# A hybrid attention, RWKV and mixture-of-experts block on one core: the output projection in another order, loads in pieces, and the experts' first weights on GpSimd's queue

## The chip, the cores and the metric

The kernel runs on one core of a Trainium2 chip. The metric is the device time of one execution in microseconds (us). It is measured from outside; a profiled execution also has a span, from its first to its last instruction, which is a little shorter than its own time.

## The reference

One layer of a streaming encoder, for 256 tokens of 2048 channels, all in float32:

```
h = rms_norm(x, g_mix);  proj = h @ w_in                       # 2048 -> 4176 + 3360 columns
y_dsa  = sparse attention (8 heads x 128): an indexer scores all keys, each query keeps
         the best 64 admissible ones, softmax over them       # head outputs h0..h7
y_rwkv = RWKV-7 (16 heads x 64): token shift, decay, delta-rule scan over the 256 tokens,
         group norm, bonus, gate                              # blocks of two heads: r0..r7
x = x + concat(y_dsa, y_rwkv) @ w_out                          # the output projection, 2048 x 2048
t = rms_norm(x, g_ffn)
route: softmax over 4 groups, the best one; softmax over its 4 experts, the best two
y = sum over the 16 experts of weight * (silu(t @ w_gate) * (t @ w_up)) @ w_down   # hidden width 512
return x + y
```

The experts' weights are 16 x 3 matrices of 4 MB, 201 MB in all. The weights of the other stages are some 80 MB.

## The kernel before

**Matmuls in two parts.** Weights come from HBM as float32. For the two big projections each 128 x 512 tile is split into a high part (ScalarE, line 205, "ACT W L205") and a low part (VectorE, line 206, "DVE W L206"), and three matmuls are made of it (high x high, high x low, low x high). All matmuls are issued on line 130, so the trace tells them apart by the tiles' names: `pp` is a bank of the two big projections, `W` the split weights, `RA` and `RB` the raw weights as loaded, `yT` the inputs of the output projection.

**The stream.** The two big projections are one list of steps, `stream`. A step takes one split tile. `drive` (line 393) walks through the list in order: it loads raw weights some steps ahead (`load_raw`, line 187, 512 KB for two steps, three places to hold them), splits them up to three steps ahead, waits until the inputs that the step needs are planned (`od.need`), and emits the step's matmuls. A step of the output projection has 6 matmuls of 128 x 512. Its list is 4 chunks of 512 output columns (cc 0 to 3) with 16 steps each; step c of a chunk takes the channels in place c of `YSLOTS`, so it needs that head's or block's output, put there by `put_y` (line 887). Each chunk holds two of the four `pp` banks from its first step to the addition of x (`u_chain`, line 1126).

**The planner.** `Order` (line 44) keeps a clock of its own, in planned TensorE time. The work beside the stream, such as the early and late part of each RWKV block, the attention and the indexer, is written as generators that give a delay or an event's name where they must wait. Between two steps of the stream `run_ready` lets every generator go on whose time has come. If a step needs something that isn't planned yet, `od.need` moves the clock forward and takes from the generators alone, with no step in between. This fixes TensorE's order of instructions. The other engines' and queues' order is made by the framework's scheduler.

**One RWKV block b.** `rwkv_early` makes the block's matrices and starts `solve` (line 645): GpSimd writes them to HBM, reads them back as `at` in another layout in one 512 KB transfer, solves in 31 pairs of instructions (lines 655 and 657), and sends the result through HBM to `XT`. `rwkv_late` (line 663) needs that, holds a lock so that only one block is in its late part, and ends in `put_y(r b)`. Block 7's late part comes last.

**The start.** xT (x transposed) is loaded in pieces on SyncE's queue, with the first weights between, then all of x in one 2 MB transfer into `xt_` (line 261). ScalarE sums the squares (line 276); the reciprocal root spread over partitions is `rsB` (made with a matmul, `rps`), by which each block's outputs are scaled in `shift`.

**The experts' weights.** They are loaded as 192 chunks of 1 MB in the order of use. The first 23 go, as memory comes free, to places that the earlier stages used: 3 in `G` after block 7's early part, 6 after block 7's late part ("rw closed"), 6 after `enter_moe` (line 1013), which follows the last step of cc 0, 4 in the places of `yT` as cc 3 comes to its end, then 1 in the raw place, 2 in the places of `W`, and the rest later. `prefetch_step` (line 1116) spreads chunks 4 to 14 over the stream: with each raw load of two steps 1/2.2 of a chunk falls due. `load_chunk(i, True)` first makes a one-element copy on GpSimd that reads the weights just split (line 1089), so that the load can't start ahead of its turn. All chunk loads are issued on SyncE (line 1092), as are the raw weights; x for the residual (`uu`, line 1011) and the router's constants are issued on GpSimd. The ring holds 20 chunks and, at first, 3 more; after that `ahead` loads a chunk each time one has been used.

**After the projection.** The router's small operations follow (lines 1191 to 1264); two of its copies are on GpSimd (lines 1223 and 1236). Then the experts, two at a time in 8 turns: `gate`, `up` and `pd` matmuls, a `sc` matmul that scatters the result, and an addition into x1, which goes out.

## Time and profile before

| | us |
|---|---|
| median of 3 runs (1102.21 to 1104.61) | 1102.25 |
| the profiled execution's own time | 1108.09 |
| its span | 1106.1 |
| TensorE busy in the span, as the records show it | 1034.8 (94%) |
| VectorE, ScalarE, GpSimd busy | 535.7, 384.0, 258.6 |
| bytes moved | 298.74 MB, 270 GB/s over the span |
| weights of the experts begin to be used | at 650.55 |

The profiled execution took 5.84 us more than the median of the runs. Matmuls are pipelined and their ends are modelled, so a busy TensorE isn't TensorE at its peak: its pace is read from how many matmuls stand in a stretch. "Granted clock" is the share of TensorE's full 2.4 GHz; 0.5 is its lower level of 1.2 GHz, and a value between is a mean over both.

### The profile page before, as it was taken

What the parts mean: (1) busy time and instruction counts of PE and PEld (TensorE: products, weight loads), DVE (VectorE), ACT (ScalarE), POOL (GpSimd) and SP (SyncE); (2) the same over time, 40 slices, a digit from 0 to 9 for tenths busy, and PEclk for the clock granted to TensorE, in tenths of its full rate; (3) what the DMA queues carried; (4) which work ended last, traced back from release to release, by engine and by line L of the source; (5) the groups of instructions that cost most, each with busy time, mean ns of one, the idle gap of its engine ahead of it and who ended that gap; (6) DMA issues with size and microseconds to landing.
All of it is one profiled execution on the core that took longest, in us unless ns stands there. A gap on an engine that the chain in (4) does not pass through costs nothing.

```text
span 1106.1 us, 17189 instructions
## 1 busy us (share of the span) xinstructions
PE 1034.8 (94%) x6466; PEld 698.7 (63%) x6466; DVE 535.7 (48%) x1193; ACT 384.0 (35%) x816; POOL 258.6 (23%) x666
## 2 busy tenths in 40 slices
PE   5999999989899999898799789999999999999996
PEld 5999888967698877686577654444444343434342
DVE  5887668777768776855354231313121313121212
ACT  6666555646446564644244211000000101010101
POOL 1416572648346535353110100000000000000000
PEclk9999999999999998998799899999999999999998
DMA  8566554454345543445299969999999999999995
GB/s 317 166 187 191 162 153 150 124 140 127 118 141 181 161 143 101 141 124 207 72 331 330 394 252 364 364 420 420 420 421 421 420 420 419 421 420 420 420 417 202
DMA packets 62266, 298.74 MB, mean 270 GB/s; under 512 B 9040, under 2 KB 12928, under 8 KB 37856
## 3 DMA queue, kind: packets, MB, share of 16 engines
q1 hardware_dynamic: 56720, 289.29, 69.6%
q0 software_dynamic: 5456, 8.28, 3.1%
q8 instruction: 53, 0.87, 0.3%
q14 instruction: 37, 0.30, 0.1%
HBM read 294.37 MB, written 3.15 MB: 269 GB/s over the span
## 4 chain that ended last, share of the span: by engine, by line
PE 77%; DMA 7%; DVE 5%; ACT 4%; POOL 3%; issue 2%; SPq 1%; ACTq 0%; DVEq 0%; POOLq 0%
PE pp L130 27%; PE pd L130 10%; PE gate L130 10%; PE up L130 10%; PE misc L130 6%; DMA RA<-wo 4%; PE sc L130 3%; PE pz L130 2%; DVE W L206 2%; PE py L130 2%; DMA xt__114<-x 1%; POOL xt L657 1%; ACT W L205 1%; POOL tt L655 1%; PE pc L130 1%
## 5 line engine op out<-in xcount | busy, mean ns | idle before, releaser
L130 PE MATMUL pp<-W,hT 128*128 128x512 f32 x768 | 194.3, 405 | 6.5 <-DVE W L206 6.5
L206 DVE TENSOR_TENSOR W<-RA,W 128x512 fp32r<-128x512 f32 x200 | 137.5, 697 | 98.9 <-ACT W L205 97.0
L130 PE MATMUL pp<-hT,W 128*128 128x256 f32 x1296 | 174.0, 292 | 11.8 <-ACT W L205 10.5
L130 PEld LDWEIGHTS pp<-hT,W 128*128 128x128 f32 x1296 | 164.5, 197 | 15.7 <-ACT W L205 10.7
L205 ACT CAST W<-RA 128x512 fp32r<-128x512 f32 x200 | 122.1, 619 | 133.5 <-PE pp L130 87.6
L130 PEld LDWEIGHTS pp<-W,hT 128*128 128x128 f32 x768 | 144.4, 193 | 38.0 <-DVE W L206 7.4
L130 PE MATMUL pp<-W,yT 128*128 128x512 f32 x384 | 99.5, 414 | 13.7 <-ACT yT L890 6.6
L655 POOL TENSOR_TENSOR tt<-xt,at 128x24 f32<-128x24 f32 (+23 forms) x248 | 89.6, 361 | 72.8 <-DMA at<-din 54.1
L130 PEld LDWEIGHTS pp<-W,yT 128*128 128x128 f32 x384 | 74.4, 198 | 34.0 <-ACT W L205 8.0
L657 POOL TENSOR_TENSOR xt<-xt,tt 128x24 f32<-128x24 f32 (+23 forms) x248 | 89.1, 359 | 19.3
L206 DVE TENSOR_TENSOR W<-RB,W 128x512 fp32r<-128x512 f32 x100 | 68.7, 695 | 38.8 <-ACT W L205 38.3
L130 PE MATMUL pd<-ew,R 128*64 128x512 f32 x352 | 81.1, 598 | 2.7 <-ACT R L1376 2.7
L205 ACT CAST W<-RB 128x512 fp32r<-128x512 f32 x100 | 61.0, 619 | 60.4 <-PE pp L130 45.5
L130 PE MATMUL up<-ew,R 128*64 128x512 f32 x352 | 79.3, 592 | 0.0
L130 PEld LDWEIGHTS misc<-sel,uu 128*128 128x128 f32 x512 | 59.6, 192 | 15.2 <-issue 13.8
L1386 ACT ACTIVATE Y<-pd,sv 128x512 fp32r<-128x512 f32 x32 | 22.0, 688 | 126.8 <-PE pd L130 126.8
L1387 DVE SCALAR_TENSOR_TENSOR Y<-pd,sv,Y 128x512 fp32r<-128x512 f32 x32 | 24.0, 751 | 83.0 <-ACT Y L1386 83.0
L130 PE MATMUL misc<-sel,uu 128*128 128x128 f32 x512 | 63.0, 278 | 0.7 <-DVE sel L1308 0.7
L1396 DVE TENSOR_TENSOR x<-x,sc 128x512 f32<-128x512 f32 x56 | 36.0, 685 | 54.9 <-PE sc L130 54.9
L130 PE MATMUL gate<-ew,R 128*64 128x512 f32 x272 | 61.7, 595 | 0.0
L1318 DVE TENSOR_TENSOR R<-misc,gF 128x512 f32<-128x512 f32 x28 | 19.4, 691 | 79.5 <-PE misc L130 79.5
L130 PEld LDWEIGHTS up<-ew,R 128*64 128x64 f32 x352 | 25.3, 137 | 50.2 <-issue 49.4
(371 smaller groups left out, 1217.2 us busy)
## 6 DMA issues: line engine op xcount, KB each, us to landing
ew<-we SPq DMA_DIRECT2D x91, 1024.0 KB, 19.1
ew<-wdn SPq DMA_DIRECT2D x40, 1024.0 KB, 17.7
ewh<-we SPq DMA_DIRECT2D x24, 1024.0 KB, 17.4
RA<-wd SPq DMA_DIRECT2D x43, 512.0 KB, 3.6
RA<-wr SPq DMA_DIRECT2D x35, 512.0 KB, 4.0
ewh<-wdn SPq DMA_DIRECT2D x12, 1024.0 KB, 19.8
RB<-wd SPq DMA_DIRECT2D x21, 512.0 KB, 3.6
RA<-wo SPq DMA_DIRECT2D x21, 512.0 KB, 6.3
```

Of the source, the lines that this page charges most:

```text
L130: PE.matmul(out, lhsT=lhsT, rhs=rhs, start=start, stop=stop, skip_group_check=skip)
L205: ACT.copy(out=hi, in_=raw)
L206: DVE.tensor_tensor(out=lo, in0=raw, in1=hi.bitcast(F32), op=ALU.subtract)
L655: POOL.tensor_tensor(out=tv, in0=xt[:, 0:n, s_:s_ + 1].broadcast_to([P, n, m]), in1=at[:, s_:s_ + 1, s_ + 1:32].broadcast_to([P, n, m]), o ...
L657: POOL.tensor_tensor(out=xt[:, 0:n, s_ + 1:32], in0=xt[:, 0:n, s_ + 1:32], in1=tv, op=ALU.subtract)
L1318: DVE.tensor_tensor(out=t, in0=ps.rearrange("p (a t) -> p a t", t=P), in1=gF[:, 4 * kq:4 * kq + 4].rearrange("p (a o) -> p a o", o=1).broa ...
L1386: ACT.activation(out=yh, in_=pd, func=AF.Copy, scale=sv[:, 1:2])
L1387: DVE.scalar_tensor_tensor(out=yl, in0=pd, scalar=sv[:, 1:2], in1=yh.bitcast(F32), op0=ALU.mult, op1=ALU.subtract)
L1396: DVE.tensor_tensor(out=x1[j][:, ns], in0=(uu[:, j, ns] if first else x1[j][:, ns]), in1=ps, op=ALU.add)
```

## The change

- `YSLOTS`: r7 moves from place 11 to the last place; the rows of `wo` follow.
- The order of the projection's steps: the first 10 of cc 0, the first 10 of cc 1, then the other 6 of cc 0 and the other 6 of cc 1 (`AHEAD` is 10). cc 2 and cc 3 stay.
- x for the first norm comes in four pieces of 512 KB, later, from a generator, into memory that the attention uses later (`yr`, `qT`); the sums of squares and `rsB` follow there. The blocks' outputs ask for `rsB` explicitly.
- The rotary tables are loaded on GpSimd's queue; `at` comes in two pieces (rows 0 to 7, and 8 to 31) into two tiles; a memset of one column is done for block 0 only; another memset goes from GpSimd to VectorE.
- Until the first turn of the experts is past its `up` matmuls (`Y2` is empty until then), chunks are issued on GpSimd's queue and not on SyncE's.
- x for cc 1 is loaded together with that for cc 0. The chunks that are due near the end of cc 3 come at its steps 7, 11 and 15 where it was 3, 7, 11 and 15.

```diff
@@ -28,7 +28,8 @@
 CLAMP = -80.0
 
 CON = [("cent", P), ("mask_s", 64), ("mask_bd", P), ("mask21", 64), ("scanm", T), ("xt0", 128), ("mu", 27), ("vecs", 64)]
-YSLOTS = ["r0", "r1", "r2", "r3", "r4", "r5", "h0", "h1", "h2", "h3", "r6", "r7", "h4", "h5", "h6", "h7"]
+YSLOTS = ["r0", "r1", "r2", "r3", "r4", "r5", "h0", "h1", "h2", "h3", "r6", "h4", "h5", "h6", "h7", "r7"]
+AHEAD = 10
 EB1, EB2, EB = 9, 4, 20
 FIRST = 1
 WARM = 19
@@ -240,7 +241,6 @@
         gT = xp.tile([P, KT], F32, name="gT")
         SP.dma_start(out=gT, in_=a["gT"])
         xT = [xp.tile([P, 4, T], F32, name=f"xT{q}") for q in range(4)]
-        xt_ = xp.tile([P, 2, D], F32, name="xt_")
 
         def load_xT(q, r0, r1):
             SP.dma_start(out=xT[q][:, r0:r1, :], in_=a["xT"][:, 4 * q + r0:4 * q + r1, :])
@@ -258,7 +258,6 @@
         load_xT(3, 0, 4)
         first[0].update(zip((4, 5), load_w(2)))
         SP.dma_start(out=ident, in_=a["ident"])
-        SP.dma_start(out=xt_, in_=a["x"].rearrange("(j p) m -> p j m", p=P))
         for q in range(4):
             for r in range(4):
                 if q == 0 and r == 1:
@@ -269,22 +268,29 @@
                 hi = hT[q][:, 0, r, :]
                 ACT.activation(out=hi, in_=xT[q][:, r, :], func=AF.Copy, scale=g)
                 DVE.scalar_tensor_tensor(out=hT[q][:, 1, r, :], in0=xT[q][:, r, :], scalar=g, in1=hi.bitcast(F32), op0=ALU.mult, op1=ALU.subtract)
-        sq = xp.tile([P, D // 2], F32, name="sq")
-        part = xp.tile([P, 2, 2], F32, name="part")
+
+    def spread():
+
+        yield 8.0
+        part = const.tile([P, 2, 2], F32, name="part")
+        xv = a["x"].rearrange("(j p) (c m) -> p j c m", p=P, c=2)
+        xs = [t.rearrange("p b t -> p (b t)").rearrange("p (c m) -> p c m", c=2) for t in (yr, qT)]
         for j in range(2):
             for c in range(2):
-                ACT.activation(out=sq, in_=xt_[:, j, c * (D // 2):(c + 1) * (D // 2)], func=AF.Square, accum_out=part[:, j, c:c + 1])
+                SP.dma_start(out=xs[j][:, c, :], in_=xv[:, j, c, :])
+                yield 1.0
+        for j in range(2):
+            for c in range(2):
+                ACT.activation(out=vt[:, j, :], in_=xs[j][:, c, :], func=AF.Square, accum_out=part[:, j, c:c + 1])
+                yield 1.0
         DVE.tensor_tensor(out=rstd, in0=part[:, :, 0], in1=part[:, :, 1], op=ALU.add)
         ACT.activation(out=rstd, in_=rstd, func=AF.Ln, scale=1.0 / D, bias=eps6)
         ACT.activation(out=rstd, in_=rstd, func=AF.Exp, scale=-0.5)
-
-    def spread():
-
-        yield RSTD_US
-        ps = pbank("rps")
         dg = temp("kd")
         for j in range(2):
             DVE.tensor_scalar(dg[:, j * P:(j + 1) * P], ident, rstd[:, j:j + 1], None, ALU.mult)
+        yield 3.0
+        ps = pbank("rps")
         mm(ps[:, 0:T], ones, dg)
         ACT.copy(out=rsB, in_=ps[:, 0:T])
         od.event("rsB", Y[22])
@@ -320,10 +326,10 @@
     def tables():
         cs128 = att.tile([P, 2, 2, 64], F32, name="cs128", tag="qr", bufs=2)
         gq = att.tile([P, 2, 128], F32, name="gq", tag="qo", bufs=2)
-        SP.dma_start(out=cs128, in_=a["cs128"])
-        SP.dma_start(out=cs64, in_=a["cs64"])
-        SP.dma_start(out=gq[:, 0, :], in_=a["q_gain"].broadcast_to([P, 128]))
-        SP.dma_start(out=gq[:, 1, :], in_=a["k_gain"].broadcast_to([P, 128]))
+        POOL.dma_start(out=cs128, in_=a["cs128"])
+        POOL.dma_start(out=cs64, in_=a["cs64"])
+        POOL.dma_start(out=gq[:, 0, :], in_=a["q_gain"].broadcast_to([P, 128]))
+        POOL.dma_start(out=gq[:, 1, :], in_=a["k_gain"].broadcast_to([P, 128]))
         for s in range(2):
             for j in range(2):
                 for hf in range(2):
@@ -506,6 +512,7 @@
             def done(ps, n=n, nm=nm):
                 if b >= 3:
                     od.need([f"early{b - 3}"])
+                od.need(["rsB"])
                 t = temp(nm)
                 st[b][nm] = t
                 shift(ps, 3 + 3 * b + n, t)
@@ -542,7 +549,8 @@
         cs = temp("e1")
         DVE.tensor_tensor_scan(cs, scanm, sa[:, 0, :], 0.0, ALU.mult, ALU.add)
         Dt = temp("Dt", 2)[:, 0:260].rearrange("p (c t) -> p c t", c=4)
-        POOL.memset(Dt[:, :, 0:1], 1.0)
+        if b == 0:
+            POOL.memset(Dt[:, :, 0:1], 1.0)
         ACT.activation(out=Dt[:, :, 1:65], in_=cs.rearrange("p (c t) -> p c t", c=4), func=AF.Exp, scale=-C0)
         di = temp("di")
         ACT.activation(out=di, in_=cs, func=AF.Exp, scale=C0)
@@ -644,16 +652,17 @@
 
     def solve(b):
 
-        at = tmp.tile([P, 32, 32], F32, name="at", bufs=1)
+        at = [tmp.tile([P, n, 32], F32, name=f"at{n}", bufs=1) for n in (8, 24)]
         xt = tmp.tile([P, 4, 32], F32, name="xt", bufs=1)
         tt = tmp.tile([P, 128], F32, name="tt", bufs=1)
-        SQ.dma_start(out=at, in_=dr[b][0].rearrange("(o ci) u s t -> o (ci u) (s t)", o=1).broadcast_to([8, 16, 1024]))
+        for t, r0, r1 in ((at[0], 0, 8), (at[1], 8, 32)):
+            SQ.dma_start(out=t, in_=dr[b][0][:, :, r0:r1, :].rearrange("(o ci) u s t -> o (ci u) (s t)", o=1).broadcast_to([8, 16, 32 * (r1 - r0)]))
         POOL.tensor_copy(xt, xt0)
         for s_ in range(31):
             n, m = s_ // 8 + 1, 31 - s_
             tv = tt[:, 0:n * m].rearrange("p (u t) -> p u t", u=n)
             POOL.tensor_tensor(out=tv, in0=xt[:, 0:n, s_:s_ + 1].broadcast_to([P, n, m]),
-                               in1=at[:, s_:s_ + 1, s_ + 1:32].broadcast_to([P, n, m]), op=ALU.mult)
+                               in1=at[s_ >= 8][:, s_ % 8 if s_ < 8 else s_ - 8, s_ + 1:32].rearrange("p (o t) -> p o t", o=1).broadcast_to([P, n, m]), op=ALU.mult)
             POOL.tensor_tensor(out=xt[:, 0:n, s_ + 1:32], in0=xt[:, 0:n, s_ + 1:32], in1=tv, op=ALU.subtract)
         SQ.dma_start(out=dr[b][1].rearrange("ci w (i q) t -> q (ci w) i t", q=8), in_=xt.rearrange("p i t -> p (i t)"))
         for ci in range(4):
@@ -869,7 +878,7 @@
                         else:
                             DVE.scalar_tensor_tensor(out=acc[:, :nk], in0=rl[:, b2, :nk], scalar=wx[:, j, hd:hd + 1], in1=acc[:, :nk], op0=ALU.mult, op1=ALU.add)
                 yield 2 * Y[17]
-            POOL.memset(acc[0:64, nk - 64:nk], NEG)
+            DVE.memset(acc[0:64, nk - 64:nk], NEG)
             for _ in range(8):
                 m8 = att.tile([P, 8], F32, name="m8", bufs=2)
                 DVE.max(m8, acc[:, :nk])
@@ -1034,6 +1043,7 @@
         xv = a["x"].rearrange("(j p) m -> p j m", p=P)
         mo_["xv"] = xv
         load_x(0)
+        load_x(1)
         for n in ("wrt", "gF", "iota", "utri", "rsum"):
             POOL.dma_start(out=mo_[n], in_=a[n])
         POOL.tensor_tensor(out=mo_["wrt"], in0=mo_["wrt"], in1=mo_["gF"].rearrange("p (k o) -> p k o", o=1).broadcast_to([P, KT, 32]), op=ALU.mult)
@@ -1052,6 +1062,7 @@
                 chunks.append(a["wdn"][2 * p + e, n])
     ring = {}
     ewp = {}
+    Y2 = []
     n_early = EB1 + 2 + EB2
     once = [EB1, EB1 + 1, n_early]
 
@@ -1088,7 +1099,10 @@
 
             POOL.tensor_copy(t[0:1, 0:1], pace["w"][0:1, 0:1].bitcast(F32))
         n = i % len(chunks)
-        if n < len(chunks) - 4:
+        if not Y2:
+
+            POOL.dma_start(out=t, in_=chunks[n])
+        elif n < len(chunks) - 4:
             SP.dma_start(out=t, in_=chunks[n])
         elif n % 2:
 
@@ -1166,16 +1180,22 @@
 
     def wo_after(cc):
         def after(c):
-            if c == 4 and cc:
+            if c == 4 and cc > 1:
                 load_x(cc)
-            if c % 4 == 3 and cc == 3:
+            if c == 7 and cc == 3:
                 while len(ring) < n_early:
                     load_chunk(len(ring), True)
+            if c % 4 == 3 and c > 3 and cc == 3:
                 load_chunk(len(ring) + 1)
+                if c == 7:
+                    load_chunk(len(ring) + 1)
         return after
 
     for cc in range(4):
         add_tm(a["wo"][cc], ybox, u_done(cc), after=wo_after(cc), needs=lambda c: [YSLOTS[c] + "y"])
+
+    c0, c1 = stream[-64:-48], stream[-48:-32]
+    stream[-64:-32] = c0[:AHEAD] + c1[:AHEAD] + c0[AHEAD:] + c1[AHEAD:]
     od.add(leave_rwkv())
     drive(prefetch_step)
     od.finish()
@@ -1283,7 +1303,7 @@
 
     x1 = []
 
-    XE, R, Y2 = [wp.tile([P, 1024], F32, name="XE", tag="rawB")], [], []
+    XE, R = [wp.tile([P, 1024], F32, name="XE", tag="rawB")], []
     load_chunk(n_early)
 
     def experts():
```

## Rows read from the trace of the kernel before

**Rows 1.** The stages around the projection and the experts: stretch, its length, busy time of TensorE, its weight loads, VectorE, ScalarE and GpSimd (with counts), the granted TensorE clock, the DMA engines' busy share, and GB/s.
```profile
515.00:547.00 32.00, 21.24 (x181) 16.47 (x180) 12.93 (x37) 11.09 (x30) 0.97 (x4) 0.79 0.18 68
547.00:562.00 15.00, 15.00 (x60) 12.21 (x60) 7.09 (x12) 6.74 (x13) 6.36 (x16) 0.89 0.87 288
562.00:587.00 25.00, 24.25 (x113) 18.62 (x112) 10.94 (x18) 11.30 (x22) 1.79 (x6) 1.00 0.95 356
587.00:614.00 27.00, 26.29 (x122) 20.27 (x122) 12.32 (x20) 11.96 (x24) 2.85 (x8) 1.00 0.92 335
614.00:637.00 23.00, 17.43 (x76) 12.78 (x74) 5.96 (x10) 5.20 (x10) 1.62 (x3) 0.85 1.01 405
637.00:651.00 14.00, 10.62 (x86) 9.01 (x88) 7.44 (x46) 3.70 (x12) 0.37 (x2) 1.00 0.65 240
651.00:707.00 56.00, 55.33 (x292) 25.15 (x290) 12.15 (x23) 4.99 (x7) 0.00 (x0) 1.00 0.87 328
707.00:1085.00 378.00, 372.39 (x1900) 163.58 (x1894) 87.79 (x162) 29.41 (x47) 0.00 (x0) 1.00 1.01 418
```

**Rows 2.** The first 30 us, in order of time: start, duration, engine, line, operation, tiles, count, and in brackets the engine's idle time before it and what ended that. SPq is SyncE issuing a transfer.
```profile
7.15 0.67 SPq L261 DMA_DIRECT2D xt__114<-x  x1
8.70 11.26 PE L130 MATMUL pp<-hT,W 128*128 128x256 f32 x66 [0.90 <-ACT hT L270]
...
13.76 0.33 SPq L193 DMA_DIRECT2D RA<-wr  x1
...
20.05 1.06 ACT L276 ACTIVATE sq<-xt__114 128x1024 f32<-128x1024 f32 x1 [3.26 <-DMA xt__114<-x]
...
23.94 1.12 ACT L205 CAST W<-RA 128x512 fp32r<-128x512 f32 x2
...
24.59 5.67 PE L130 MATMUL pp<-hT,W 128*128 128x256 f32 x31 [4.64 <-ACT W L205]
```

**Rows 3.** TensorE in order of time around the first steps of the projection: the first and the last of the six groups of its matmuls before block 7's output is there (66 matmuls in all: 6, 18, 24, 6, 6, 6), and the first group after it.
```profile
491.68 1.55 PE L130 MATMUL pp<-W,yT 128*128 128x512 f32 x6
...
522.72 2.71 PE L130 MATMUL pp<-W,yT 128*128 128x512 f32 x6 [3.38 <-ACT yT L890]
...
546.71 19.67 PE L130 MATMUL pp<-W,yT 128*128 128x512 f32 x78 [3.27 <-ACT yT L890]
```

**Rows 4.** The chain of work that ended last, in order of time: start, length, what.
```profile
514.96 2.28 PE py L130 x32
...
537.06 4.38 PE py L130 x32
...
546.71 12.88 PE pp L130 x48
...
562.96 8.74 DMA RA<-wo
...
614.70 13.11 DMA RA<-wo
...
650.55 3.65 PE gate L130 x16
```

**Rows 5.** The projection after block 7's output: first the group of its matmuls from 546 to 637 (busy, mean ns of one, idle before and what ended it), then three rows in order of time: a stretch of it without waits, its last long wait, and the first addition of x.
```profile
L130 PE MATMUL pp<-W,yT 128*128 128x512 f32 x318 | 80.6, 409 | 10.3 <-ACT W L205 6.4 <-ACT yT L890 3.3 <-DVE W L206 0.7
```
```profile
603.82 12.79 PE L130 MATMUL pp<-W,yT 128*128 128x512 f32 x54
...
628.56 6.26 PE L130 MATMUL pp<-W,yT 128*128 128x512 f32 x18 [5.55 <-ACT W L205]
```
```profile
554.85 0.69 DVE L1131 TENSOR_TENSOR uu<-uu,pp 128x512 f32<-128x512 f32 x1 [0.69 <-PE pp L130]
```

**Rows 6.** Transfers by tile: queue, count, KB of each, median us from issue to landing. The first four are of the whole span, the fifth of 548 to 557 alone.
```profile
RA<-wd SPq DMA_DIRECT2D x43, 512.0 KB, 3.6
...
RA<-wo SPq DMA_DIRECT2D x21, 512.0 KB, 6.3
...
at<-din POOLq DMA_DIRECT2D x8, 512.0 KB, 7.3
...
uu<-x POOLq DMA_DIRECT2D x4, 512.0 KB, 7.9
```
```profile
uu<-x POOLq DMA_DIRECT2D x1, 512.0 KB, 4.8
```

**Rows 7.** GpSimd in order of time: a load of x as GpSimd issues it, and the first of the router's two copies.
```profile
562.70 0.74 POOL L1011 DMA_DIRECT2D uu<-x  x1 [0.18 <-POOL ew L1089]
...
642.78 0.18 POOL L1223 COPY ps<-lp 128x8 f32<-128x8 f32 x1 [26.86 <-ACT lp L1218]
```

**Rows 8.** The end of the experts: SyncE's last weight load, the transfers of that kind (256 KB pieces), and the last matmuls with weights in the chain.
```profile
1083.94 0.33 SPq L1098 DMA_DIRECT2D ew<-wdn  x1
```
```profile
ew<-wdn SPq DMA_DIRECT2D x16, 256.0 KB, 6.2
```
```profile
1094.64 1.92 PE pd L130 x8
```

**Rows 9.** The solves: the only wait of TensorE for a solve's result, in order of time; and two rows of GpSimd's waits over the span (total us, times, longest).
```profile
129.91 1.54 PE L130 MATMUL pz<-R,XT 128*128 128x128 f32 x8 [2.49 <-DMA XT<-dout]
```
```profile
POOL tt L655 <- DMA at<-din: 54.1, 8, 7.8
POOL G L545 <- DVE G L569: 46.7, 4, 24.2
```

## The prediction

> **What bounds the kernel now.** I read the table by stretches first, then TensorE and the chain of waits in the stretches that stand out, then the transfers, and last the end.
>
> From 707 on the DMA engines are full at 418 GB/s while TensorE has next to no gap [rows 1]; the first matmul on an expert's weight is at 650.55 and the last ends at 1094.64 + 1.92 = 1096.56 [rows 4, 8]. In these 446 us TensorE uses 192 chunks, one in 2.32 us; at 418 GB/s a chunk of 1.049 MB takes 2.51 us. So the experts are paced by TensorE only because some 20 chunks are there when they begin. To start them earlier is worth its full amount as long as that lead lasts.
>
> Where can the start come earlier? From 515 to 547 TensorE is busy 21.24 of 32 us at a granted clock of 0.79, with DMA at 0.18 [rows 1]: the planner has no step left but that of r7, and r7's late part runs alone. Only 66 matmuls of the projection, 11 steps, stand before r7's output at 546.71 [rows 3]. The low clock shows in the same 32 `py` matmuls: 2.28 us for block 6, 4.38 us for block 7 [rows 4]. Then come 53 steps, to about 637, and in them TensorE waits 7.0 us besides the first 3.3 for r7 [rows 5]. The long ones are raw weights that land late: 13.11 us for 512 KB at 614.70, where SyncE's queue also holds chunks [rows 4]. At the start, TensorE stands 4.64 us at 24.59 behind a split whose ScalarE stood behind the 2 MB of x, and whose weight load, issued at 13.76, was behind them in the queue as well [rows 2].
>
> **The change part by part.** The sum is made against the profiled execution's own 1108.09 us.
>
> *The order of the projection.* With r7 last and 10 steps of cc 1 put forward, 25 steps (20, and r6 and h4 to h7 of cc 0) don't need r7, where it was 11. 14 steps move ahead of r7. A step without waits costs 6 x 12.79/54 = 1.42 us [rows 5], so 19.9 us of work leave the stretch behind r7, and 39 steps stay there: 55.4 us, and some 4 us for transposes and the router's matmuls in between.
>
> What do they cost ahead of r7? The gaps from 515 to 547 are 32 - 21.24 = 10.8 us [rows 1]. A mean clock of 0.79 is 42% of the time at the lower level, 13.4 us; if TensorE is busy in two thirds of that, full speed gives back 4.5 us (2.1 of them in `py` [rows 4]). At best the 14 steps cost 19.9 - 10.8 - 4.5 = 5 us there. At worst each pushes the chain of r7 by its whole length, 20 us. The chain is some nine stages with waits between, and a step that is under way delays a stage by 0.7 us on average: 6 us. I take r7 7 us later, near the lower end, as the gaps are measured.
>
> A new wait: cc 0 and cc 1 now hold all four banks, so cc 2 can't begin before x is added to cc 0, and cc 1's end needs the whole chain of cc 0 planned, with no step in between. r7's step and the 6 of cc 1 take 10 us from r7's output; x for cc 0 landed 4.8 us after its issue [rows 6] and was added 8.1 us after r7 [rows 4, 5]. Bounds 0 and 6 us (x landing 7.9 us after its issue, as the median, behind a chunk). I take 3; behind it all 32 steps of cc 2 and 3 would stand.
>
> *The chunks on GpSimd's queue.* Raw weights no longer stand behind 1 MB chunks. A raw load of the same size took 3.6 us in the first projection and 6.3 in this one [rows 6]. If that comes back the 7.0 us of waits go; at worst they stay, since the bytes are the same. I take 6. Issuing costs GpSimd 0.74 us for each [rows 7], some 36 times, beside nothing else but the router's copies; for the first three chunks, which fall into block 7's solve, it is 2 us on that solve, between 0 and 2 on r7; it is in the 7.
>
> Here the Trainium skill speaks against the change. "DMA: Bandwidth & Descriptors", section "Issuing engines are not separate DMA queues", says that transfers from all queues run on the same 16 engines, and that more issuing engines save only the issue time. By that alone the waits stay and the time is 6 us above mine (rival 5). The rows speak for more, 13.11 us against 3.6 for one size; the rule doesn't exclude this, since it is about bandwidth and not about who stands behind whom.
>
> *The start.* Without the 2 MB the load issued at 13.76 finds no x ahead of it, and ScalarE no wait: the 4.64 us go. The four pieces come back later, 2 MB beside weights of at least 128 GB/s (512 KB for two steps of 24 matmuls, at 11.26/66 us each [rows 2]). So the wait could come back in full, or all go, or, with more transfers in the way than now, grow by its own length: -4.6 to 4.6. I take 4.5, the gap that the row shows, since the first blocks' outputs can wait for the sums in their banks. It carries on because TensorE is what later stages wait for, and its order there stays nearly the same.
>
> *The solve in two pieces, memsets, tables.* GpSimd waits 54.1 us for `at` in 8 solves, and TensorE for a solve only once, 2.49 us [rows 9]. A first piece of a quarter saves at most three quarters of 7.3 us a solve [rows 6], one more issue costs 0.7 [rows 7]. GpSimd's waits of 46.7 us before the memset cover only its own idle time. Value -0.7 to 2.5; I take 1. The later chunks of cc 3 and the four table loads I put at 0, with 1 us either way.
>
> Sum: the 14 steps give 19.9, less 7 and 3: 9.9. The waits give 6. The 39 steps at full clock give another 4: before, 318 matmuls took 90.3 - 7.0 - 4 = 79.3 us, 1.50 us a step and not 1.42, over 53 steps. Start 4.5, solve 1. In all 25.4 us, so 1108.09 - 25.4 = 1082.7 for a profiled execution. That execution took 5.84 us more than the median of the runs; from 1102.25 it is 1077 us.
>
> **Does DMA allow it?** The last weight load is issued at 1083.94 and lands by about 1089, needed by 1094.64 [rows 8]: 5 us free. Between 547 and 707 the engines fell short of 420 GB/s by 4.7 + 3.8 + 5.5 + 0.8 + 6.0 + 12.3 = 33 us [rows 1]. The 14 steps moved ahead of r7 take 3.7 MB, 8.7 us, with them. So the loads could end 47 us earlier if nothing were left unused. With the start of the experts pulled in, most of the 18 us lost from 637 to 707 (full buffers) go; the paced stretch keeps some 10, and the beginning 5. That leaves room for about 30 us. My 25 fit, barely, and much more than 30 can't come.
>
> **The rivals.**
> 1. *The DMA becomes the bound of the experts.* If the projection gets faster but the loads stay as thin as before, 33 us unused, only 5 + 8.7 = 14 us can be had: 1088 us, with TensorE waiting for weights in the last turns. For it: the lead is spent almost to the end even now. Against: the 12.3 us after 651 came from full buffers.
> 2. *r7 is pushed back by all that is put ahead of it.* The 14 steps gain nothing, and the waits and the start remain: 1102.25 - 6 - 4.5 = 1092 us. For it: ScalarE and VectorE must split each step's weights, and r7's chain runs through the same two. Against: they are busy 11 and 13 of 32 us there [rows 1].
> 3. *Slower: GpSimd's queue can't feed the experts.* Some 36 chunks, 37.7 MB, go over it. Chunk 38 is used at 650.55 + 38 x 2.32 = 739 now. From 547 that asks for 37.7 MB in 192 us: below 196 GB/s this queue starts a delay that nothing makes up, as the DMA engines have no time to spare later. At 180 GB/s it is 209 us, 17 us later: 1119 us. For it: `at` over this queue took 7.3 us for 512 KB, twice SyncE's 3.6. Against: x for cc 0 took 4.8 for the same size [rows 6]. The Trainium skill has a rule that points this way: "SBUF — State Buffer", section "SBUF: two separate sides", warns that a copy on VectorE in its two-port mode keeps GpSimd from writing descriptors. No run here shows that yet.
> 4. *The change doesn't do what it says.* The planner places the new steps so that r7 stays the end, and the pieces of x hold ScalarE as the whole did: within 3 us of 1102.
> 5. *The raw loads wait as long as before*, since the chunks take their share of the same engines: the 6 us stay, 1083 us. For it: 405 GB/s were moved in the stretch with the longest wait. Against: 288 to 356 in the ones before, with waits as well [rows 1].
>
> **How the numbers follow.** The forecast, 1077 with its own range 1064 to 1087, has 0.42; rival 1 has 0.15, rival 2 0.15, rival 3 0.13, rival 4 0.05, rival 5 0.10. A difference under 0.3% (3.3 us) can't be told from none. Faster by more: forecast, rivals 1, 2 and 5, 0.82. Within: 0.05. Slower: 0.13. The range holds the forecast's own and reaches to rivals 1 and 2 with the bounds of r7's delay: 1064 to 1096.
>
> **What would show it.** Right: no gap of TensorE near 20 us; 150 matmuls of `pp<-W,yT` before r7's output, and a granted clock near 1 from 515 on; about 39 steps behind it in some 64 us; raw loads of `wo` landing in 4 to 6 us; the first `gate` matmul at about 625; and no waits of TensorE for `ew` until the end. Wrong: r7's output later than 555 (rival 2), TensorE waiting for chunks in the last turns (rival 1) or in the first two (rival 3), or a wait at the head of cc 2 of over 6 us.

## The result, and the profile of the changed kernel

| | before | changed |
|---|---|---|
| median, us | 1102.26 | 1066.91 (4 runs, 1065.43 to 1069.68) |
| ratio | 1 | 0.9677, interval 0.9654 to 0.9701 |
| the profiled execution, us | 1108.09 | 1065.43 |
| first `gate` matmul, in the trace | 650.55 | 607.98 |

The change makes the kernel 35.3 us faster. The forecast was 25 us, 1077 with a range of 1064 to 1096; the time lies in the range, 3 us above its lower end, and the rivals of no gain and of a loss are out. The gain is larger than forecast, though, and the rest of this document shows that the sum came out right in total for one half of the change and wrong for the other.

The stages of the changed kernel, in the columns of [rows 1]:

```profile
515.00:547.00 32.00, 25.57 (x181) 19.70 (x178) 14.60 (x27) 13.08 (x31) 8.62 (x20) 0.89 0.53 169
547.00:562.00 15.00, 15.00 (x72) 12.39 (x71) 6.77 (x10) 7.77 (x14) 4.42 (x7) 1.00 0.89 333
562.00:587.00 25.00, 25.00 (x120) 20.13 (x119) 11.59 (x19) 11.86 (x22) 9.13 (x20) 1.00 0.95 354
587.00:600.00 13.00, 10.95 (x66) 7.29 (x65) 4.41 (x14) 4.65 (x13) 2.65 (x5) 1.00 1.02 426
...
614.00:637.00 23.00, 23.00 (x126) 10.35 (x124) 2.90 (x10) 1.66 (x2) 4.21 (x8) 1.00 1.01 420
637.00:651.00 14.00, 13.32 (x80) 6.85 (x78) 2.79 (x4) 1.27 (x2) 1.58 (x3) 1.00 0.98 405
651.00:707.00 56.00, 55.32 (x286) 24.54 (x284) 13.59 (x25) 4.40 (x7) 0.00 (x0) 1.00 0.99 400
707.00:1040.00 333.00, 328.07 (x1664) 143.12 (x1662) 79.33 (x144) 26.47 (x43) 0.00 (x0) 1.00 1.01 419
```

The DMA engines are full or nearly so from 587 on (400 GB/s and more), where before they were full from 707 on. The granted clock is 1.00 from 547 on; before, 614 to 637 had 0.85. In the first 8 us from r7's step on it is low in both kernels; the first row is of the kernel before, the second of the changed one:

```profile
546.70:554.00 7.30, 7.29 (x25) 5.87 (x26) 2.33 (x4) 1.86 (x3) 4.91 (x14) 0.75 0.86 288
```
```profile
532.00:540.00 8.00, 7.93 (x25) 6.37 (x26) 2.50 (x4) 1.88 (x4) 6.30 (x17) 0.71 0.80 274
```

TensorE in order of time: the first step of the projection, r7's, the head of cc 2, the only other wait for weights, and the first matmul of the experts. Below it the last `pd` of the chain of waits.

```profile
470.97 3.01 PE L131 MATMUL pp<-W,yT 128*128 128x512 f32 x12
...
532.07 11.96 PE L131 MATMUL pp<-W,yT 128*128 128x512 f32 x42 [3.27 <-ACT yT L899]
...
545.76 0.64 PE L131 MATMUL pl<-uT,wrt 128*32 128x256 f32 x8 [0.85 <-issue]
...
590.85 1.43 PE L131 MATMUL pp<-W,yT 128*128 128x512 f32 x5 [0.23 <-DVE W L207]
...
607.98 3.65 PE L131 MATMUL gate<-ew,XE 128*64 128x512 f32 x16 [0.78 <-DVE XE L1338]
```
```profile
1052.11 1.92 PE pd L131 x8
```

Three distances tell where the time went. The projection begins at 470.97 and not at 491.68 [rows 3]: 20.7 us are gained before the projection is touched. From there to the first `gate` matmul it was 158.9 us and is 137.0, another 21.9. From the first `gate` to the end of the last `pd` it was 446.0 us [rows 4, 8] and is the same to 0.1 us: the experts are paced as before, and what they gain is their earlier start. In every experiment below this last distance is 446.0 as well, but in e1 (448.2). (These distances come from one execution of each kernel, and that of before took 5.8 us more than its median.)

Transfers by tile, as in [rows 6]:

```profile
ew<-we POOLq DMA_DIRECT2D x25, 1024.0 KB, 10.6
RA<-wo SPq DMA_DIRECT2D x21, 512.0 KB, 4.1
RB<-wo SPq DMA_DIRECT2D x11, 512.0 KB, 5.1
at<-din POOLq DMA_DIRECT2D x8, 384.0 KB, 6.3
uu<-x POOLq DMA_DIRECT2D x4, 512.0 KB, 6.0
...
at<-din POOLq DMA_DIRECT2D x8, 128.0 KB, 3.6
```

The raw weights of the projection land in 4.1 and 5.1 us where `RA` took 6.3 and `RB` 6.8. The first piece of `at` lands in 3.6 us where the whole took 7.3.

### The profile page after: what moved, and what is told of

Read it like the earlier page. It is cut to its first block, busy times and chain, and to the rows that moved or that the text cites. A ratio compares the mean times of both kernels' runs of the same rounds, so it can differ in the third digit from the quotient of the medians.

```text
span 1063.3 us, 17241 instructions
## 1 busy us (share of the span) xinstructions
PE 1015.9 (96%) x6466; PEld 685.3 (64%) x6466; DVE 536.6 (50%) x1195; ACT 386.4 (36%) x816; POOL 287.2 (27%) x705
## 4 chain that ended last, share of the span: by engine, by line
PE 73%; DVE 4%; ACT 2%; issue 1%; DMA 1%; ACTq 0%; DVEq 0%
PE pp L131 23%; PE pd L131 11%; PE gate L131 11%; PE up L131 10%; PE misc L131 6%; PE sc L131 3%; PE pz L131 2%; PE py L131 2%; DVE W L207 1%; DMA RB<-wo 1%; ACT W L206 1%; PE pc L131 1%; PE lps L131 1%; PE yps L131 1%; PE misc L141 1%
## 5 line engine op out<-in xcount | busy, mean ns | idle before, releaser
L131 PE MATMUL pp<-W,hT 128*128 128x512 f32 x768 | 189.7, 398 | 1.6 <-DVE W L207 1.6
L131 PE MATMUL pp<-hT,W 128*128 128x256 f32 x1296 | 171.6, 289 | 12.3 <-ACT W L206 8.6
L131 PEld LDWEIGHTS pp<-hT,W 128*128 128x128 f32 x1296 | 161.7, 194 | 17.1 <-ACT W L206 8.8
L131 PEld LDWEIGHTS pp<-W,hT 128*128 128x128 f32 x768 | 141.2, 189 | 32.1 <-DVE W L207 2.0
L131 PE MATMUL pp<-W,yT 128*128 128x512 f32 x384 | 95.5, 403 | 3.5 <-ACT yT L899 3.3
L666 POOL TENSOR_TENSOR xt<-xt,tt 128x24 f32<-128x24 f32 (+23 forms) x248 | 91.8, 370 | 19.3
L664 POOL TENSOR_TENSOR tt<-xt,at 128x24 f32<-128x24 f32 (+23 forms) x248 | 86.0, 347 | 40.0 <-DMA at<-din 21.3
L131 PEld LDWEIGHTS pp<-W,yT 128*128 128x128 f32 x384 | 72.1, 192 | 20.7 <-ACT yT L899 3.5
L1349 ACT CAST selT<-misc 128x256 fp32r<-128x256 f32 x8 | 3.0, 372 | 154.5 <-PE misc L131 154.5
## 6 DMA issues: line engine op xcount, KB each, us to landing
ew<-we SPq DMA_DIRECT2D x66, 1024.0 KB, 19.9
```

The costliest lines, as they stand in the source:

```text
L131: PE.matmul(out, lhsT=lhsT, rhs=rhs, start=start, stop=stop, skip_group_check=skip)
L664: POOL.tensor_tensor(out=tv, in0=xt[:, 0:n, s_:s_ + 1].broadcast_to([P, n, m]), in1=at[s_ >= 8][:, s_ % 8 if s_ < 8 else s_ - 8, s_ + 1:32 ...
L666: POOL.tensor_tensor(out=xt[:, 0:n, s_ + 1:32], in0=xt[:, 0:n, s_ + 1:32], in1=tv, op=ALU.subtract)
L1349: ACT.copy(out=selT, in_=ps[:, 0:T])
```

## The experiments

All times are medians. Each kernel is given as a ratio to runs of the kernel before on the same chip, since that kernel's median moved between 1101.9 and 1103.8 from one group of runs to the next. A difference of two ratios is uncertain by some 0.35 to 0.45%, 4 to 5 us. "From the changed kernel" and "from the kernel before" say on which the edit is made.

### The projection: its order, the queue and the place of the chunks

**e11: the whole projection half, on the kernel before.** The edits to `YSLOTS`, `stream`, `load_x`, `Y2` and `wo_after` from the diff above; the start, the solve, the memsets and the tables stay.

> The kernel before with all that the change does to the projection and to the chunks (order, x for cc 1, chunks on GpSimd's queue, the later burst), and nothing of the start, the solve, the memsets and the tables. By the terms of the prediction (14 steps less r7's delay and the wait 9.9, raw loads 6, clock 4) it gains 20 us: ratio 0.982. If the projection's part was right as the trace of the changed kernel has it, the gain is 18 to 24 us, ratio 0.978 to 0.984, first gate matmul at 622 to 632. If the parts of the stream and of the projection need each other (the single undoings add up to 29 of 35 us), it gains under 15 us, ratio above 0.986.

Measured: 1081.74 us, ratio 0.9816 (0.9787 to 0.9845), a gain of 20.3 us; first `gate` at 623.58. The sum had 9.9 + 6 + 4 = 19.9. The changed kernel stands 0.9816 - 0.9677 = 1.39%, 15.3 us, below this one: that is what the stream half brings on top, and the sum had 4.5 + 1 for it. This kernel's trace is also a second execution of the old stream: its projection begins at 485.76, 14.8 us after that of the changed kernel.

```profile
485.76 1.55 PE L131 MATMUL pp<-W,yT 128*128 128x512 f32 x6
```

**e1: the old order, in the changed kernel.**

```diff
-YSLOTS = ["r0", "r1", "r2", "r3", "r4", "r5", "h0", "h1", "h2", "h3", "r6", "h4", "h5", "h6", "h7", "r7"]
+YSLOTS = ["r0", "r1", "r2", "r3", "r4", "r5", "h0", "h1", "h2", "h3", "r6", "r7", "h4", "h5", "h6", "h7"]
-    c0, c1 = stream[-64:-48], stream[-48:-32]
-    stream[-64:-32] = c0[:AHEAD] + c1[:AHEAD] + c0[AHEAD:] + c1[AHEAD:]
```

> The changed kernel with the old YSLOTS and without the reordering of steps; all else of the change stays. My sum: the projection's order is worth 9.9 + 4 us of the 25, and with the gaps that the changed trace no longer has some 20: about 1085 us, r7's output again with 11 steps ahead of it and TensorE gaps of 10 us before it. Rival (the order gains nothing, r7 is pushed back by what is put ahead): about 1067 us, as the changed kernel.

Measured: 1079.74 us, 0.9782 (0.975 to 0.9814): the order is worth 1.05%, 11.6 us, with the rest in place, where the expectation had some 18. Both kernels reach the projection within 0.5 us of each other, so their traces give the parts: r7's step comes at 523.2 with 11 steps ahead of it and at 532.07 with 25, 8.9 us later; what follows it ends at 606.7 and at 594.45.

```profile
523.20 19.60 PE L131 MATMUL pp<-W,yT 128*128 128x512 f32 x78 [3.27 <-ACT yT L899]
```

**e2: the order alone, on the kernel before.** The lines of e1 the other way, and x for cc 1 loaded with that for cc 0:

```diff
         load_x(0)
+        load_x(1)
...
-            if c == 4 and cc:
+            if c == 4 and cc > 1:
```

> The kernel before with the new order alone (and x for cc 1 loaded with that for cc 0, which the order needs). Chunks stay on SyncE's queue. My sum: 14 to 20 us of the 35, about 1084 to 1088 us. If raw loads behind chunks hold the projection more the faster it is, less: 1095 us.

Measured: 1101.32 us, 0.999 (0.9963 to 1.0018): no gain, outside what was expected. r7 has 25 steps ahead of it, as wanted, and two waits take it all back. The first stands ahead of r7: ScalarE waits 3.37 us for a raw load that SyncE issued right behind a chunk, VectorE and TensorE stand behind ScalarE, and the granted clock is 0.81 from 496 to 510. r7's step comes 66.7 us after the first of the projection, where it is 61.2 in e11. The second is the long one, behind r7:

```profile
493.66 0.66 PE L131 MATMUL pq<-MM,WG 128*64 128x128 f32 x8 [2.03 <-DVE sm L909]
...
620.40 6.41 PE L131 MATMUL pp<-W,yT 128*128 128x512 f32 x18 [13.91 <-ACT W L206]
```

SyncE in order of time shows what it stands behind. First the kernel before, ahead of the load that took 13.11 us [rows 4]; then e2:

```profile
611.20 0.33 SPq L1092 DMA_DIRECT2D ewh<-wdn  x1
613.66 0.93 SPq L1092 DMA_DIRECT2D ew<-we  x2
614.70 0.36 SPq L193 DMA_DIRECT2D RA<-wo  x1
```
```profile
594.66 0.33 SPq L1094 DMA_DIRECT2D ewh<-wdn  x1
595.80 0.93 SPq L1094 DMA_DIRECT2D ewx<-we  x2
596.78 3.22 SPq L1094 DMA_DIRECT2D ew<-we  x4
600.10 0.50 SPq L194 DMA_DIRECT2D RA<-wo  x1
```

At step 3 of cc 3 `wo_after` issues every early chunk that isn't issued yet, and one more; this is the burst. Before, 3 chunks of 1 MB went ahead of the raw load; with the new order it is 7, as 14 fewer steps follow r7 over which they could be spread. The wait grows from 5.55 us [rows 5] to 13.91. So the order needs something else from the change. Three runs tell what.

**e3: the chunks on SyncE's queue, in the changed kernel;** the later place of the burst stays.

```diff
-        if not Y2:
+        if False:
```

> The changed kernel with the chunks on SyncE's queue again. My sum: 6 us slower, about 1073 us, with raw loads of wo landing in 6 us and TensorE waiting some 7 us for split weights in the projection. By the rule that queues share the same engines: no difference, 1067 us.

Measured: 1070.64 us, 0.9698 (0.9666 to 0.973), 0.2% or 2.3 us behind the changed kernel, between the two that were expected and less than the uncertainty. TensorE has one wait of 1.75 us for weights at 590.91, and no long one.

**e9: the old place of the burst, on GpSimd's queue, in the changed kernel.**

```diff
-            if c == 7 and cc == 3:
+            if c % 4 == 3 and cc == 3:
                 while len(ring) < n_early:
                     load_chunk(len(ring), True)
-            if c % 4 == 3 and c > 3 and cc == 3:
                 load_chunk(len(ring) + 1)
-                if c == 7:
-                    load_chunk(len(ring) + 1)
```

> The changed kernel with the chunks at the end of cc 3 where they were before: the burst at its step 3, and one chunk at steps 3, 7, 11 and 15; all of them on GpSimd's queue. Theory A (what removed the stall of 13.9 us of the order alone is that raw loads no longer stand behind the chunks in SyncE's queue): no wait of TensorE over 2 us in cc 3, and a time within 0.3% of the changed kernel, ratio 0.966 to 0.970. Theory B (the later place of the burst removed it, the queue doesn't matter): a wait of 8 to 14 us near the start of cc 3 comes back, ratio 0.974 to 0.981.

Measured: 1079.88 us, 0.9794 (0.9764 to 0.9824), 1.17% or 12.9 us slower than the changed kernel. The time is what theory B expected and its wait isn't there: in the projection TensorE waits nowhere over 0.25 us for weights, and the projection's matmuls end at 595.01, as in the changed kernel at 594.45. Yet the first `gate` comes at 621.81. GpSimd and VectorE in order of time, and the chain of waits, show a third thing:

```profile
581.15 0.53 POOL L1104 DMA_DIRECT2D ewh<-wdn  x1 [0.60 <-PE pp L131]
585.91 0.72 POOL L1020 DMA_DIRECT2D uu<-x  x1 [4.23 <-DMA ewx<-we]
```
```profile
605.50 1.29 DVE L1145 TENSOR_TENSOR uu<-uu,pp 128x512 f32<-128x512 f32 x2 [13.55 <-DMA uu<-x]
```
```profile
585.91 19.47 DMA uu<-x
```

x for cc 3 is loaded at step 4 on GpSimd's queue. The burst at step 3 on the same queue, with one chunk of step 7 eight transfers of 1 MB, is now ahead of it. GpSimd issues the load only at 585.91, after the first of the eight has landed, and the 512 KB then take 19.47 us; before, with no chunks on that queue, such a load landed in 7.9 us [rows 6]. The chunks that moved queue moved past `load_x`, and the later place in `wo_after` puts them behind it: there the same load is issued at 577.30, ahead of the burst, and lands in 10.65 us.

**e10: the old place on SyncE's queue, in the changed kernel:** the edits of e3 and e9 together.

> As e9, with the chunks on SyncE's queue: what is left of the change is the order and the parts of the stream. Theory A (queue): the stall of 10 to 14 us is back early in cc 3, the first gate matmul comes at 620 to 626, ratio 0.974 to 0.984, 7 us or more above e9. Theory B (place): the same stall, but e9 has it too. If neither the queue nor the place matters here (the stall of the order alone was chance): no wait over 2 us, ratio 0.967 to 0.971.

Measured: 1083.71 us, 0.9824 (0.9794 to 0.9855), 1.26% or 13.9 us behind e3, which differs in the place alone. The stall is the one of e2, behind 7 chunks again:

```profile
602.31 6.58 PE L131 MATMUL pp<-W,yT 128*128 128x512 f32 x18 [13.80 <-ACT W L206]
```

So both theories on e9 held half: the queue decides who stands behind the burst (raw weights, or x), and the place decides whether anyone does. With the new place the queue is worth 2.3 us, with the old one 0.30%, 3.3 us, both within the uncertainty; the place is worth 13 us on either queue. The two raw loads that were issued beside the burst in e9, on SyncE's queue at 576.82 and 579.54, landed in 9.3 and 10.4 us, where x, as large, took 19.5 behind it. This agrees with what the Trainium skill says in "DMA: Bandwidth & Descriptors", section "Queues, rings and completion order": each DMA engine takes turns between the queues that have work for it.

### The stream before the projection

**e12: `at` in two pieces, alone, on the kernel before.**

```diff
-        at = tmp.tile([P, 32, 32], F32, name="at", bufs=1)
+        at = [tmp.tile([P, n, 32], F32, name=f"at{n}", bufs=1) for n in (8, 24)]
...
-        SQ.dma_start(out=at, in_=dr[b][0].rearrange("(o ci) u s t -> o (ci u) (s t)", o=1).broadcast_to([8, 16, 1024]))
+        for t, r0, r1 in ((at[0], 0, 8), (at[1], 8, 32)):
+            SQ.dma_start(out=t, in_=dr[b][0][:, :, r0:r1, :].rearrange("(o ci) u s t -> o (ci u) (s t)", o=1).broadcast_to([8, 16, 32 * (r1 - r0)]))
```

> The kernel before with at in two pieces and nothing else. By the prediction: 1 us faster, ratio 0.999 (bounds 0.9977 to 1.0006). If the 7.8 us that the whole at costs in the changed kernel are the solve's own (two waits of TensorE for XT, and the stream's order behind them): 5 to 9 us faster, ratio 0.992 to 0.9955. If they come from the order that the planner and the waits happen to make in the changed kernel: within 0.2% of the kernel before.

Measured: 1090.23 us, 0.9887 (0.9859 to 0.9914): 12.5 us from an edit that the sum put at 1 us, more than any of the three expectations. The order of TensorE's instructions is that of the kernel before but for one matmul, so nothing was planned differently; the same waits became shorter. Waits of GpSimd and of VectorE from 60 to 500, the kernel before and then e12:

```profile
POOL tt L655 <- DMA at<-din: 54.1, 8, 7.8
```
```profile
DVE m L875 <- POOL acc L872: 11.8, 2, 6.9
```
```profile
POOL tt L656 <- DMA at<-din: 21.9, 8, 4.4
```
```profile
DVE m L876 <- POOL acc L873: 2.0, 2, 1.6
```

GpSimd waits 54.1 - 21.9 = 32.2 us less, 4 us a solve. One way by which this reaches TensorE, besides its direct wait of 2.49 us [rows 9], is seen in the kernel before at 290, on GpSimd, VectorE and TensorE:

```profile
286.84 2.20 POOL L660 DMA_DIRECT2D XT<-dout  x4 [2.86 <-PE pp L130]
289.04 0.30 POOL L651 COPY xt<-con 128x128 f32<-128x128 f32 x1
289.27 0.17 POOL L872 MEMSET acc<- 64x64 f32 x1
```
```profile
289.47 0.43 DVE L875 MAX8 m<-acc 128x8 f32<-128x256 f32 x1 [6.86 <-POOL acc L872]
289.82 0.67 DVE L206 TENSOR_TENSOR W<-RB,W 128x512 fp32r<-128x512 f32 x1
```
```profile
290.54 4.37 PE L130 MATMUL pp<-W,hT 128*128 128x512 f32 x11 [4.37 <-DVE W L206]
```

The memset of `acc` takes 0.17 us, but in GpSimd's list a solve and the loads of its result stand ahead of it. VectorE waits 6.86 us for it at the search for the best keys (`MAX8`), with the split of the next weights next in its list, and TensorE waits 4.37 us for that split. At 236 the same happens for 3.76 us, with another result of VectorE (`MM`) in the split's place. How long these two waits are depends on the execution: 11.8 us on VectorE in the trace of before, and 5.6 in that of e11, whose stream is the same.

How much of the 12.5 us comes by this way isn't shown by e12 itself. Its projection begins here, 8.1 us ahead of e11's:

```profile
477.69 1.55 PE L130 MATMUL pp<-W,yT 128*128 128x512 f32 x6
```

Of these 8.1 us some 2 come at the direct wait near 130 and some 1.5 at the wait behind the memset near 283; the rest is spread over smaller steps. Another 3.9 us come in the projection (155.0 us to the first `gate`, and 158.9 before). What the memset alone is worth is what e5 shows.

**e5: the memset of `acc` on VectorE, alone, on the kernel before.**

```diff
-            POOL.memset(acc[0:64, nk - 64:nk], NEG)
+            DVE.memset(acc[0:64, nk - 64:nk], NEG)
```

> The kernel before with one word changed: the memset of acc on VectorE. Theory A: 8 to 12 us faster than before, about 1092 us, and TensorE's waits of 3.76 and 4.37 us at 236 and 290 are gone. Theory B: within 3 us of 1102.

Measured: 1098.01 us, 0.9961 (0.9938 to 0.9983), 4.3 us, between the two theories. The waits for `acc` are gone from the trace. With 2.5 us for the direct wait (3.6 in e5's trace) that accounts for 7 to 8 of e12's 12.5 us; where the rest comes from stays open.

**e4: the memset back on GpSimd, in the changed kernel** (the line of e5 the other way).

> The changed kernel with the memset of acc on GpSimd again, nothing else. In the kernel before it stood on GpSimd behind the solve's waits and held VectorE for 4.95 and 6.86 us, after which TensorE waited 3.76 and 4.37. Theory A (this memset is most of the 20 us gained ahead of the projection): 7 to 12 us slower, about 1076 us, with VectorE waits for acc of 10 us. Theory B (that gain comes from the planner's other order and the solve's pieces): under 3 us, about 1068 us.

Measured: 1068.76 us, 0.9681 (0.9654 to 0.9708): nothing. Theory A, by which this memset carried most of what the stream gained, falls. With a shorter solve there is little left to wait for: VectorE waits 0.8 us for `acc` here. The two edits remove the same wait.

**e6: `at` in one transfer again, in the changed kernel** (the lines of e12 the other way).

> The changed kernel with at in one transfer again. My sum: TensorE waits for a solve once, about 2.5 us slower, 1069 us. Rival (each solve's 3 us add up, as the late parts wait for the solves): 8 us or more slower, 1075 us.

Measured: 1074.35 us, 0.9748 (0.972 to 0.9775), 0.71% or 7.8 us slower, as the rival to the sum had it. Here, with the memset gone from the path, TensorE waits for the solve's results, twice, 4.5 us in all; the other 3.3 are not in any single wait:

```profile
132.68 1.13 PE L131 MATMUL pz<-R,XT 128*128 128x128 f32 x8 [1.91 <-DMA XT<-dout]
...
289.94 1.13 PE L131 MATMUL pz<-R,XT 128*128 128x128 f32 x8 [2.59 <-DMA XT<-dout]
```

**e7: x in one 2 MB transfer at the start, in the changed kernel.** The sums of squares stand at the start again, and `spread` begins with its old delay.

```diff
+        SP.dma_start(out=xt_, in_=a["x"].rearrange("(j p) m -> p j m", p=P))
...
-                SP.dma_start(out=xs[j][:, c, :], in_=xv[:, j, c, :])
...
-                ACT.activation(out=vt[:, j, :], in_=xs[j][:, c, :], func=AF.Square, accum_out=part[:, j, c:c + 1])
+                ACT.activation(out=sq, in_=xt_[:, j, c * (D // 2):(c + 1) * (D // 2)], func=AF.Square, accum_out=part[:, j, c:c + 1])
```

> The changed kernel with x for the first norm in one 2 MB transfer at the start again. The changed trace is only 1 us ahead at 55 us of its span, so the pieces gain about 1 us: 1068 us. By my sum, which gave the start 4.5 us: 1071 to 1072 us.

Measured: 1075.83 us, 0.9746 (0.9721 to 0.9771), 0.69% or 7.6 us slower, more than either expectation. The stall at the start comes back, but most of it is made up: e7 is 7.6 us behind at the 100th of the stream's matmuls (24 us in the changed kernel), 2.4 at the 700th (120 us) and 2.0 at the 1800th (371 us), no more than another execution with the changed start (e4) is behind there, 2.8 us. The loss that stays appears between the 1870th and the 1900th, around 400 us, where it goes to some 8 us; at the first step of the projection it is 7.2. In e7, and not in the changed kernel, TensorE has these waits there:

```profile
402.11 0.46 PE L131 MATMUL lps<-kT,qT 128*128 128x128 f32 x2 [2.16 <-DVE MM L605]
403.04 0.67 PE L131 MATMUL lps<-kT,qT 128*128 128x256 f32 x2 [0.47 <-DVE MM L605]
405.42 0.90 PE L141 MATMUL ptp<-ident,L 128*128 128x128 f32 x3 [1.71 <-DVE R L692]
```

The order of TensorE's instructions differs between these two kernels: `rsB` is planned at another time, and the planner places the work of the later blocks otherwise. That this different order makes the loss is the likeliest reading; no run moved the planned time by itself. The profiled execution of e7 took 4.3 us more than its median, and 7 us more than the changed kernel from the projection's first step to the first `gate`, so its trace places more loss than the median has.

**e8: the one-column memset for every block, in the changed kernel.**

```diff
-        if b == 0:
-            POOL.memset(Dt[:, :, 0:1], 1.0)
+        POOL.memset(Dt[:, :, 0:1], 1.0)
```

> The changed kernel with the one-column memset of Dt on GpSimd for every block again. My sum puts it at 0: 1067 us. Rival (it holds GpSimd, and by that the sigmoid or the solve, for up to 24 us each time): 3 to 8 us slower, 1070 to 1075 us.

Measured: 1066.99 us, 0.9666 (0.9642 to 0.9691): nothing, as forecast.

**The account.** The projection half alone is 20.3 us and the stream half on top of it 15.3. Undone singly, the parts of the stream half cost 7.8 (solve) + 7.6 (start) + 0.4 (acc) + 0 (the one-column memset): 15.8. Each of these is uncertain by 4 us, and on the kernel before the parts are worth something else (12.5 for the solve, 4.3 for `acc`), so that the sum comes so near is partly luck. The tables were not tried by themselves.

## Why the prediction came out as it did

**What bounds the kernel.** Right. The start of the experts moved by 42.6 us in the traces and the end of the last `pd` by 42.5.

**The order, 19.9 - 7 - 3.** Right in the sum, 9.9 against 11.6 in e1, within the uncertainty. Its parts were off by some 2 us each way: r7 was pushed back by 8.9 us, not 7; behind it 21.1 us went and not 19.9; and the new wait, put at 3 us, is 0.85 at the head of cc 2. Rival 2, all 20 us given back, is out.

**Full clock, 4.** Mostly wrong. Ahead of r7 the clock did come back in part: the `py` group of block 7 takes 2.58 us, not 4.38 [rows 4], and the stretch from 515 has 0.89 instead of 0.79. But the 4 us were counted behind r7, and there the clock falls as before: TensorE is busy for 3.38 us of the 8 ahead of r7's step, and from 532 to 540 the granted clock is 0.71, where it was 0.75 from 546.70 to 554. The 234 matmuls behind r7 keep TensorE busy for 58.1 us, 1.49 us a step; before, it was 80.6 us [rows 5] for 318, 1.52 a step. Over 39 steps that is 1.2 us, not 4. All in all the 39 steps took 594.45 - 532.07 = 62.4 us, and the forecast's some 64 came near it because the wait at cc 2 was put 2 us too high while the full clock failed to come.

**The raw loads' waits, 6, by the queue.** The waits went (7.0 us before, 0.23 now) and the loads land in 4 to 5 us, but the step gave them to the wrong line of the diff. The queue is worth 2 to 3 us, which the uncertainty doesn't tell from none. The forecast said that "the later chunks of cc 3 and the four table loads I put at 0, with 1 us either way"; the place of these chunks is worth 13 us once the order is changed. Two things were missed: that the new order leaves 7 chunks for the burst where there were 3, and that on GpSimd's queue the burst can stand ahead of `load_x`. Rival 5 had the queue about right: the rule of the Trainium skill that it rests on ("DMA: Bandwidth & Descriptors", section "Issuing engines are not separate DMA queues"), that transfers from all queues share the same engines, fits the 2.3 us of e3. What that rule doesn't speak of, who is behind whom on one queue, is the 13 us.

**The start, 4.5, and why it lasts.** The direct gap went (the changed kernel has 1.90 us in its place, at 28.76), but the lead is mostly gone by the 700th matmul, so the forecast's "It carries on because TensorE is what later stages wait for, and its order there stays nearly the same" is wrong on both counts. The 7.6 us of e7 stand elsewhere, around 400 us, with another order of TensorE. So the sum has a gain for the start by a reason that the runs don't bear out.

**The solve, 1, between -0.7 and 2.5.** This is the term that failed most, outside its own bounds: 7.8 us in the changed kernel, 12.5 alone. The step read only TensorE's direct wait for a solve, 2.49 us [rows 9], as what could be won. In the changed kernel with the whole `at` there are two such waits, 4.5 us (e6). And the sentence "GpSimd's waits of 46.7 us before the memset cover only its own idle time" took the memsets to be harmless. One of them wasn't: the memset of `acc`, which had no row and no price, stood behind the solve, VectorE behind the memset, and TensorE behind VectorE. VectorE's list of waits, with 11.8 us for a 0.17 us memset, would have shown this path; the forecast read GpSimd's list and TensorE's, and not the one in between. That path is worth 4.3 us on the kernel before (e5) and nothing in the changed one (e4); some 5 us of the 12.5 and some 3 of the 7.8 no run traces to a wait.

**The DMA's room.** "Much more than 30 can't come" was too tight: 35.3 came, and 42.6 between the two traces. Against 420 GB/s the engines fall short by 3.1 + 3.9 + 0.5 + 2.7 = 10 us between 547 and 707, by the rows of stages above, where it was 33; the forecast kept some 10 + 5 us for that, about right. But it counted from a fixed 547, and the stream brought r7 14.6 us and the first chunk around it 14.0 us forward as well (546.3 to 532.3). The last weight load is issued here at 1041.79, 42.2 us earlier, and TensorE waits for no chunk. Rivals 1 and 3 are out: GpSimd's queue and SyncE's together moved 419 to 426 GB/s from 587 to 637, and an issue of a chunk took 0.53 us.

So the time came out 10 us below the forecast because the stream half was worth 15.3 and not 5.5, while the projection half, 20.3 against 19.9, held only in total: the raw loads' price stood on the wrong line, and the clock's 4 us, of which 1.2 came, was made good by the order and the waits. That it holds to 0.4 us is luck.

## What to carry to other kernels

A short instruction can be as late as the longest thing ahead of it on its engine, as the memset was behind the solve: read the waits of each engine between the slow work and the bound, and ask of a solve or a transfer that becomes shorter who is queued behind it, not only who uses its result. When transfers move to another queue or another time, list by time what each queue then holds; here the same burst of seven chunks cost 13 us ahead of a raw load on one queue, 13 us ahead of x on the other, and next to nothing four steps later. And an edit tried alone can be worth nothing (the order), or 4 us that are nothing beside another edit that removes the same wait (the memset), so the account needs the halves as well as the single lines.

## What was not expected of the hardware

In e9 a transfer took the time of what was ahead of it on its queue, and not of its size: 512 KB landed after 19.47 us behind 1 MB chunks on GpSimd's queue, and two loads of the same size, issued beside the burst on SyncE's queue, after 9.34 and 10.38 us. The DMA engines moved 361 GB/s from 576 to 590 and 422 from 585 to 606. And `at` is slow for its size: 512 KB took 7.3 us in the kernel before, where `wd`'s 512 KB land in 3.6 [rows 6]. In pieces it takes 3.6 us for 128 KB and 6.3 for 384 KB, but the second piece is issued some 0.6 us behind the first on the same queue, so its time holds part of the first's.
